# A layer kernel on one core: feed-forward weight steps to and fro, factors through the step, early first units of the next phases

## The chip, the cores and the metric

The kernel runs on one core of a Trainium2 chip. A core has TensorE (PE, matrix products; PEld is its loading of weights), VectorE (DVE), ScalarE (ACT), GpSimd (POOL) and SyncE (SP), which in this kernel issues nearly all transfers. Engines run their own instructions in order and wait for each other by semaphores; an engine's transfers go out in the order in which it issues them. The metric is the device time of one launch in microseconds (us), lower is better.

## The reference

One inference step of a layer: 2048 new tokens behind 16 meta tokens, and 8 running sequences of 4 tokens. Two branches (a state space layer, a gated delta rule) are merged and projected, and a dense gated channel mixer follows. The change concerns the merge's end and what comes after it, in float32:

```
mix = (sigmoid(ga) * br_a + sigmoid(gb) * br_b) @ w_out
x = x + rms_norm(mix, norm_mix_post)
f = rms_norm(x, norm_ffn_pre)                      # 2080 tokens x 1024
f = (silu(f @ w_ffn_gate) * (f @ w_ffn_up)) @ w_ffn_down     # 1024 -> 2816 -> 1024
x = x + rms_norm(f, norm_ffn_post)
```

## The kernel before, in words

Every product of two float32 matrices is made as three products: each operand is split in a rounded part (`xh`, `ah`, `wh`, `hh`, by an ACT copy) and a rest (`xl`, `al`, `wl`, `hl`, by a DVE or POOL subtraction), and hi by hi, lo by hi and hi by lo are summed in PSUM (`mm3`, lines 157 to 159).

The stages, in time: the input projection and the two branches; the merge (`p2_products`), which writes `mg_d` in memory; the way out (`way_out`: `way_rows` multiplies with `w_out`, `way_tail` normalises, adds, normalises again, writes `y_prompt` and has `to_dram` transpose the rows, `pst`, and write them to `f_d` in column form, `fo`); gate and up (`gate_up`), which reads `f_d` as `fr` and writes the gated product to `h_d`; and down, which reads `h_d` as `hr` and `w_ffn_down` as `wr` (`wload`), and sums in `psr`. In the way out, a group is two row tiles of 128 tokens.

Gate and up takes the tokens in three pairs of column blocks (348, 348 and 344 wide, `PAIRS`) and, for each, the weights in 11 steps of 256 columns. A step makes two 2 by 2 block products (gate, i = 0, and up, i = 1) with seven block products each instead of eight, from sums and differences of blocks, in the order a11, a12, s2, s1, s3, a22, s4. A block product is 4 times three matmuls, so a step is 2 x 7 x 12 = 168 matmuls on tiles `psf`.

- `b_parts` loads the four blocks of a token pair (`fr`), forms t1 to t4 on DVE and splits seven operands: eleven DVE operations on 128x1392. For the next pair it is a generator that the last step of a pair advances at its `more()` calls. Its results have one buffer each.
- `a_parts` loads two weight blocks of 1 MB for a step (`araw`, two buffers), forms s1 to s4 on DVE (`S`) and splits: of each matrix a11/a12 and s2/s1 on DVE, s3/s4 and a22 on POOL. It is called for the next step before a step's own code; the split factors lie in a ring of 50 KB a partition (`ar`).
- `gate_up_step`: `sn` is an ACT copy of a product that is needed later, `su` a DVE sum, `th` the tanh gate (ACT, then DVE), `hm` the gated product (mostly POOL), stored by SP.

A scheduler places the instructions, by the order in which the code emits them and by its own estimates; the order on an engine is therefore not that of the text. Pools with `reuse_waits="tile"` may lie over memory of an earlier stage: a tile waits for what lay there.

Down has, for each half of the tokens, four groups of 6, 6, 5 and 5 row blocks of `w_ffn_down`; a block is loaded into one of two `wr` buffers, its rounded half made by ACT, the two halves of the rest by POOL and DVE (lines 142, 144, 145).

The pools around the change, before:

```
                self.tm = self.pool("tm2", 3, ph, **kw)
...
            self.ar = ar.ring(50 * 1024, name="ar")
            self.ar.tile([P, 3072], F32, name="pad")
...
            self.wr = self.pool("wr3", 2, ph, **kw)
            self.wp.add(self.pool("wp3", 12, ph, **kw), 12)
```

Of the kernel before, what the change touches and what calls it, by code (L numbers as in the profile page):

```python
# [7 lines left out]
F32 = mybir.dt.float32  # L8
# [7 lines left out]
P = 128  # L16
# [54 lines left out]
class Trunk:  # L71
# [57 lines left out]
    def wload(self, parts, eng=0):  # L129

        nc = self.nc
        hi = self.wp.tile([P, 1024], F32R, tag="wh", name="wh")
        lo = self.wp.tile([P, 1024], F32R, tag="wl", name="wl")
# [135 lines left out]
    def to_dram(self, ys, gain):  # L269
# [4 lines left out]
        for k0 in range(0, 8, 2):  # L274
# [8 lines left out]
            nc.sync.dma_start(ap_of(self.f_d, k0 * P * XW + c0, [[XW, P], [P * XW, 2], [1, w]]), ft[:, :, :w])  # L283
# [988 lines left out]
    def p2_products(self, b, prep, part, ws):  # L1272
# [4 lines left out]
        for q in range(2):  # L1277
# [27 lines left out]
            nc.sync.dma_start(ap_of(self.mg_d, r0 + b * BLK, [[XW, P], [1, BLK]]), tb[:, 0:BLK])  # L1305
            if b == 0:
                nc.sync.dma_start(ap_of(self.mg_d, r0 + SEQ, [[XW, P], [1, SMP]]), tb[:, BLK:BLK + SMP])
# [116 lines left out]
    def b_parts(self, c0, w):  # L1424
# [7 lines left out]
        def parts(nm, t):  # L1432
            pool = self.xp if nm in ("b11", "b21") else self.xq
# [29 lines left out]
    def a_parts(self, s):  # L1463

        nc, v, gp = self.nc, self.nc.vector, self.nc.gpsimd
        out = [{}, {}]
        def parts(i, names, x, eng):
# [3 lines left out]
            hf, lf = [t.rearrange("p a k m -> p (a k) m") for t in (hi, lo)]  # L1471
            nc.scalar.activation(hf, x, AF.Copy)  # L1472
            eng.tensor_sub(lf, x, hf.bitcast(F32))  # L1473
            for j, nm in enumerate(names):
                out[i][nm] = hi[:, j], lo[:, j]
        raws = []
        for i, w in enumerate((self.w_fg, self.w_fu)):
            raw = self.gr.tile([P, 8, 256], F32, tag="raw", name="araw")
            nc.sync.dma_start(raw, ap_of(w, 256 * s, [[FF, P], [P * FF, 8], [1, 256]]))
            parts(i, ("a11", "a12"), raw[:, :, 0:P], v)  # L1480
            raws.append(raw)
        sums = []
        for i, raw in enumerate(raws):
            a, c = raw[:, :, 0:P], raw[:, :, P:256]
            S = self.gs.tile([P, 4, 4, P], F32, tag="S", name="S")
            v.tensor_add(S[:, 1], c[:, 0:4], c[:, 4:8])  # L1486
            v.tensor_sub(S[:, 2], a[:, 0:4], c[:, 0:4])
            v.tensor_sub(S[:, 0], S[:, 1], a[:, 0:4])  # L1488
            v.tensor_sub(S[:, 3], a[:, 4:8], S[:, 0])
            sums.append(S.rearrange("p a k m -> p (a k) m"))  # L1490
            parts(i, ("s2", "s1"), sums[i][:, 0:8], v)
        for i, raw in enumerate(raws):
            parts(i, ("s3", "s4"), sums[i][:, 8:16], gp)
            parts(i, ("a22",), raw[:, 4:8, P:256], gp)
        return out

    def gate_up(self):
        nc, v = self.nc, self.nc.vector
        xs = self.b_parts(*PAIRS[0])
        B = None  # L1500
        for B in xs:
            pass
        A = self.a_parts(0)
        last = FF // 256 - 1
        for pi, (c0, w) in enumerate(PAIRS):
# [424 lines left out]
```

## Time and profile before

| | |
|---|---|
| median of 3 runs | 3311.0 us (3310.6 to 3314.44) |
| profiled execution | 3310.43 us, span 3308.7 us |
| mean clock of PE | 0.975 |
| PE busy | 3112.5 us (94%) |
| last matmul of the way out's products | starts at 1802 us |
| gate and up, first to last matmul | 1822.7 to 2777.0 us |
| down, first matmul | 2787.1 us |

Times are counted from the span's start. A row in time has its start, its length, the engine, the line, the operation, the tiles (out<-in) and, in brackets, how long the engine had been idle before it and what released it. A row of a group has the number of instructions after x, their summed time, the mean of one in ns, and the idle time before them. `SPq` and `POOLq` are issues of transfers by these engines.

### The profile page before, as it was taken

How to read it: one execution, taken by the hardware profiler on the slowest of the kernel's cores; microseconds unless marked ns; L12 is line 12 of the kernel's file. 1: busy time of each engine (PE TensorE's matmuls, PEld its weight loads, DVE VectorE, ACT ScalarE, POOL GpSimd, SP SyncE). 2: the span in 40 equal slices, each digit the busy share in tenths (PEclk: the TensorE clock that was granted, in tenths of full speed). 3: DMA queues.
4: the chain of work that ended last, by engine and by line, in shares of the span. 5: the costliest groups of instructions: out<-in, count | busy, mean ns of one | idle time of the engine just before them, and what ended most of it. 6: DMA issues, size and time to landing. Idle time of an engine off the chain costs nothing. (4 is left out here: it accounts for less than half of the span.)

```text
span 3308.7 us, 47381 instructions
## 1 busy us (share of the span) xinstructions
PE 3112.5 (94%) x17461; PEld 2721.0 (82%) x17461; DVE 2078.1 (63%) x4672; ACT 1125.2 (34%) x1960; POOL 888.5 (27%) x835
## 2 busy tenths in 40 slices
PE   6998999999999998999998799999999998999998
PEld 5887878877777777988776799999989997888886
DVE  6888854657887546553454767777776774236235
ACT  4633222433332224221243434434443443313211
POOL 1123431123232212101000344444453443212110
PEclk9999999999999999999999899999999999999999
DMA  5336465545465435653553423343332334326223
GB/s 117 122 100 183 118 171 163 123 119 148 143 193 161 125 111 162 194 153 125 160 186 139 141 95 104 107 136 103 103 100 85 107 110 131 123 86 163 78 64 69
DMA packets 483224, 423.48 MB, mean 128 GB/s; under 512 B 122906, under 2 KB 407642, under 8 KB 482992
## 3 DMA queue, kind: packets, MB, share of 16 engines
q1 hardware_dynamic: 478288, 403.42, 41.3%
q0 software_dynamic: 4704, 17.04, 2.3%
q8 instruction: 137, 2.24, 0.3%
q14 instruction: 95, 0.78, 0.1%
HBM read 292.46 MB, written 127.65 MB: 127 GB/s over the span
## 5 line engine op out<-in xcount | busy, mean ns | idle before, releaser
L157 PE MATMUL psf<-xh,ah 128*128 128x348 f32 (+1 forms) x1848 | 603.6, 327 | 35.4 <-ACT sn L1525 30.8
L159 PE MATMUL psf<-xh,al 128*128 128x348 f32 (+1 forms) x1848 | 597.6, 324 | 17.0 <-DVE al L1473 17.0
L158 PE MATMUL psf<-xl,ah 128*128 128x348 f32 (+1 forms) x1848 | 595.7, 322 | 0.0
L144 POOL TENSOR_TENSOR wl<-wr,wh 128x512 fp32r<-128x512 f32 x136 | 221.8, 1634 | 892.0 <-ACT wh L142 811.0
L157 PEld LDWEIGHTS psf<-xh,ah 128*128 128x128 f32 x1848 | 350.7, 190 | 49.5 <-ACT sn L1525 44.3
L159 PEld LDWEIGHTS psf<-xh,al 128*128 128x128 f32 x1848 | 350.6, 190 | 18.5 <-DVE al L1473 18.5
L158 PEld LDWEIGHTS psf<-xl,ah 128*128 128x128 f32 x1848 | 350.7, 190 | 0.0
L157 PE MATMUL psg<-pgh,wh 128*128 128x512 f32 (+1 forms) x800 | 301.0, 376 | 1.3 <-ACT wh L142 1.3
L1621 PE MATMUL psr<-wh,hh 128*128 128x512 f32 (+2 forms) x748 | 291.2, 391 | 9.8 <-ACT wh L142 9.8
L159 PE MATMUL psg<-pgh,wl 128*128 128x512 f32 (+1 forms) x800 | 291.6, 365 | 4.9 <-DVE wl L145 4.1
L1622 PE MATMUL psr<-wl,hh 128*128 128x512 f32 (+2 forms) x748 | 292.3, 391 | 3.0 <-POOL wl L144 3.0
L158 PE MATMUL psg<-pgl,wh 128*128 128x512 f32 (+1 forms) x800 | 292.1, 365 | 0.0
L1624 PE MATMUL psr<-wh,hl 128*128 128x512 f32 x704 | 274.3, 390 | 0.0
L142 ACT ACTIVATE wh<-wr 128x1024 fp32r<-128x1024 f32 x136 | 143.1, 1056 | 256.8 <-PE psg L158 58.9
L1473 POOL TENSOR_TENSOR al<-S,ah 128x1024 fp32r<-128x1024 f32 x66 | 162.8, 2467 | 228.4 <-ACT ah L1472 130.8
L145 DVE TENSOR_TENSOR wl<-wr,wh 128x512 fp32r<-128x512 f32 x136 | 114.8, 845 | 147.3 <-ACT wh L142 146.5
L1472 ACT ACTIVATE ah<-araw 128x1024 fp32r<-128x1024 f32 (+1 forms) x132 | 110.7, 840 | 224.6 <-DMA araw<-w_ffn_up 106.2
L1472 ACT ACTIVATE ah<-S 128x1024 fp32r<-128x1024 f32 x132 | 135.8, 1051 | 142.2 <-DVE S L1488 124.3
L157 PE MATMUL psq<-pgh,wh 128*128 128x512 f32 (+1 forms) x480 | 181.9, 379 | 0.4 <-ACT pgh L264 0.3
L159 PEld LDWEIGHTS psg<-pgh,wl 128*128 128x128 f32 x800 | 156.1, 195 | 31.1 <-issue 4.6
L157 PEld LDWEIGHTS psg<-pgh,wh 128*128 128x128 f32 x800 | 156.4, 196 | 24.7 <-issue 3.6
L158 PEld LDWEIGHTS psg<-pgl,wh 128*128 128x128 f32 x800 | 156.5, 196 | 22.0 <-issue 2.6
(490 smaller groups left out, 6826.6 us busy)
## 6 DMA issues: line engine op xcount, KB each, us to landing
wr<-w_in SPq DMA_DIRECT2D x72, 512.0 KB
araw<-w_ffn_gate SPq DMA_DIRECT2D x33, 1024.0 KB
araw<-w_ffn_up SPq DMA_DIRECT2D x33, 1024.0 KB
wr<-w_ffn_down SPq DMA_DIRECT2D x44, 512.0 KB
zg_d<-gt SPq DMA_DIRECT2D x80, 256.0 KB
h_d<-hm SPq DMA_DIRECT2D x44, 348.0 KB
qkv_d<-cy SPq DMA_DIRECT2D x48, 256.0 KB
hr<-h_d SPq DMA_DIRECT2D x16, 768.0 KB
```

What stands on the lines that cost most here:

```text
L142: nc.scalar.activation(hi[:, :n], raw[:, :n], AF.Copy)
L144: nc.gpsimd.tensor_sub(lo[:, :c], raw[:, :c], hi[:, :c].bitcast(F32))
L145: nc.vector.tensor_sub(lo[:, c:n], raw[:, c:n], hi[:, c:n].bitcast(F32))
L157: t.matmul(ps, wh, xh, start=first, stop=False, **kw)
L158: t.matmul(ps, wh, xl, start=False, stop=False, **kw)
L159: t.matmul(ps, wl, xh, start=False, stop=last, **kw)
L1472: nc.scalar.activation(hf, x, AF.Copy)
L1473: eng.tensor_sub(lf, x, hf.bitcast(F32))
L1621: nc.tensor.matmul(ps, hi[:, k, cl], wh[:, cs], start=k == 0, stop=False)
L1622: nc.tensor.matmul(ps, hi[:, k, cl], wl[:, cs], start=False, stop=both and k == n - 1)
L1624: nc.tensor.matmul(ps, lo[:, k, c - c0:c - c0 + r], wh[:, cs], start=False, stop=k == n - 1)
```

## The change

- The stores of the way out to `f_d` and of the merge to `mg_d` are issued by GpSimd instead of SP.
- The pairs pass over the weight steps to and fro: 0 to 10, 10 to 0, 0 to 10. At a change of pair the step is the same, and its factors are kept: `a_parts` runs 31 times instead of 33.
- `a_parts` is a generator that the step advances by `fac()` at six places, with what is left at the step's end. `S` of four blocks becomes `S` (s2, s1) and `R` (s3, s4).
- Pools: `su` has 3 buffers instead of 4, `th` 2 instead of 3, the ring `ar` 56 KB instead of 50 with 24 KB of padding instead of 12, `tm2` 4 buffers instead of 3; t1 and t2 have a pool of their own (`xr`).
- Down's pools lie otherwise: `wr` and ten of the `wh` and `wl` pairs (now one tile, `wu`) on the right side, over memory of `ar`, `araw` and others; two pairs, `hh` and `hr` on the left.

How the order moves, at three places. New lines carry numbers 3 to 16 higher for the same code. On DVE, from the last rows of the way out (`wa`) into the first step: the splits of the first token pair (`xl`, with `fr` and `t` for the sums) and of the first two factors (`al<-araw` of gate and up). Before:

```order
L1407 TENSOR_SCALAR wa<-xr,wrs 128x1024 x2
L1486 TENSOR_TENSOR S<-araw 128x512
L1487 TENSOR_TENSOR S<-araw 128x512
L1488 TENSOR_TENSOR S<-S,araw 128x512
L1489 TENSOR_TENSOR S<-araw,S 128x512
L1446 TENSOR_TENSOR fr<-fr 128x1392
L1473 TENSOR_TENSOR al<-araw,ah 128x1024
L1449 TENSOR_TENSOR t_17730<-fr 128x1392
L1437 TENSOR_TENSOR xl<-fr,xh 128x1392
```

And the rows that follow it, up to the second `al`:

```order
L1454 TENSOR_TENSOR fr<-fr 128x1392
L1437 TENSOR_TENSOR xl<-t_17730,xh 128x1392
L1437 TENSOR_TENSOR xl<-fr,xh 128x1392 x2
L1458 TENSOR_TENSOR t_17730<-fr,t_17730 128x1392
L1473 TENSOR_TENSOR al<-araw,ah 128x1024
```

After:

```order
L1411 TENSOR_SCALAR wa<-xr,wrs 128x1024 x2
L1450 TENSOR_TENSOR fr<-fr 128x1392
L1453 TENSOR_TENSOR t_17733<-fr 128x1392
L1441 TENSOR_TENSOR xl<-fr,xh 128x1392
L1458 TENSOR_TENSOR fr<-fr 128x1392
L1441 TENSOR_TENSOR xl<-t_17733,xh 128x1392
L1441 TENSOR_TENSOR xl<-fr,xh 128x1392 x2
L1462 TENSOR_TENSOR t_17733<-fr,t_17733 128x1392
L1476 TENSOR_TENSOR al<-araw,ah 128x1024 x2
```

The first `al` stood between the token operations and stands behind them now; four operations on `S` and `R` have moved ahead, in among the roots of the last rows.

On POOL, one plain step of the first pair, from the `hm` that ends the step before. Before:

```order
L1576 TENSOR_TENSOR hm<-th,su 128x348
L1473 TENSOR_TENSOR al<-S,ah 128x1024
L1473 TENSOR_TENSOR al<-araw,ah 128x512
L1551 TENSOR_TENSOR hm<-th,su 128x348
L1564 TENSOR_TENSOR hm<-th,su 128x348
L1473 TENSOR_TENSOR al<-S,ah 128x1024
L1473 TENSOR_TENSOR al<-araw,ah 128x512
```

After:

```order
L1589 TENSOR_TENSOR hm<-th,su 128x348
L1476 TENSOR_TENSOR al<-R,ah 128x1024
L1562 TENSOR_TENSOR hm<-th,su 128x348
L1576 TENSOR_TENSOR hm<-th,su 128x348
L1476 TENSOR_TENSOR al<-araw,ah 128x512
L1476 TENSOR_TENSOR al<-R,ah 128x1024
L1476 TENSOR_TENSOR al<-araw,ah 128x512
```

Three of the four splits now stand behind the step's own `hm` and one ahead of them. A weight buffer is free after its `al<-araw`, so the loads' issues move to the end of a step.

On SP, the end of gate and up and the first loads of down. Before:

```order
L1479 DMA araw<-w_ffn_up 128x8x256
L1538 DMA h_d<-hm 128x688 x2
L1732 DMA row<-norm_ffn_post 128x1024
L1538 DMA h_d<-hm 128x688
L1605 DMA hr<-h_d 128x6x256
L1538 DMA h_d<-hm 128x688
L1605 DMA hr<-h_d 128x6x256
L140 DMA wr<-w_ffn_down 128x1024 x2
L1605 DMA hr<-h_d 128x6x256 x2
L140 DMA wr<-w_ffn_down 128x1024 x8
```

After:

```order
L1482 DMA araw<-w_ffn_up 128x8x256
L1547 DMA h_d<-hm 128x688 x2
L144 DMA wr<-w_ffn_down 128x1024
L1547 DMA h_d<-hm 128x688 x2
L144 DMA wr<-w_ffn_down 128x1024
L1621 DMA hr<-h_d 128x6x256 x2
L1547 DMA h_d<-hm 128x688
L1750 DMA row<-norm_ffn_post 128x1024
L1547 DMA h_d<-hm 128x688
L144 DMA wr<-w_ffn_down 128x1024 x8
```

Two loads of weights and two of `hr` have moved ahead of the last two stores of `h_d`; the other weights stay behind them.

The diff, cut:

```diff
...
-    def wload(self, parts, eng=0):
+    def wload(self, parts, one=False):
         nc = self.nc
-        hi = self.wp.tile([P, 1024], F32R, tag="wh", name="wh")
-        lo = self.wp.tile([P, 1024], F32R, tag="wl", name="wl")
+        if one:
+            both = self.wp.tile([P, 2, 1024], F32R, tag="wu", name="wu")
+            hi, lo = both[:, 0], both[:, 1]
+        else:
+            hi = self.wp.tile([P, 1024], F32R, tag="wh", name="wh")
+            lo = self.wp.tile([P, 1024], F32R, tag="wl", name="wl")
         raw = self.wr.tile([P, 1024], F32, tag="wr", name="wr")
...
                 nc.scalar.activation(ft[:, kt - k0, :w], ps[:, kt - k0, :w], AF.Copy, scale=gain[:, kt:kt + 1])
-            nc.sync.dma_start(ap_of(self.f_d, k0 * P * XW + c0, [[XW, P], [P * XW, 2], [1, w]]), ft[:, :, :w])
+            nc.gpsimd.dma_start(ap_of(self.f_d, k0 * P * XW + c0, [[XW, P], [P * XW, 2], [1, w]]), ft[:, :, :w])
             yield
...
             r0 = m * P * XW
-            nc.sync.dma_start(ap_of(self.mg_d, r0 + b * BLK, [[XW, P], [1, BLK]]), tb[:, 0:BLK])
+            nc.gpsimd.dma_start(ap_of(self.mg_d, r0 + b * BLK, [[XW, P], [1, BLK]]), tb[:, 0:BLK])
             if b == 0:
-                nc.sync.dma_start(ap_of(self.mg_d, r0 + SEQ, [[XW, P], [1, SMP]]), tb[:, BLK:BLK + SMP])
+                nc.gpsimd.dma_start(ap_of(self.mg_d, r0 + SEQ, [[XW, P], [1, SMP]]), tb[:, BLK:BLK + SMP])
             yield
...
         def parts(nm, t):
-            pool = self.xp if nm in ("b11", "b21") else self.xq
+            pool = self.xp if nm in ("b11", "b21") else self.xr if nm in ("t1", "t2") else self.xq
             hi = pool.tile([P, 4, GW], F32R, tag=nm + "h", bufs=1, name="xh")[:, :, :w]
...
-    def a_parts(self, s):
+    def a_parts(self, s, out):
         nc, v, gp = self.nc, self.nc.vector, self.nc.gpsimd
-        out = [{}, {}]
+        flat = lambda t: t.rearrange("p a k m -> p (a k) m")
         def parts(i, names, x, eng):
...
             lo = self.ar.tile([P, n, 4, P], F32R, name="al")
-            hf, lf = [t.rearrange("p a k m -> p (a k) m") for t in (hi, lo)]
-            nc.scalar.activation(hf, x, AF.Copy)
-            eng.tensor_sub(lf, x, hf.bitcast(F32))
+            nc.scalar.activation(flat(hi), x, AF.Copy)
+            eng.tensor_sub(flat(lo), x, flat(hi).bitcast(F32))
             for j, nm in enumerate(names):
                 out[i][nm] = hi[:, j], lo[:, j]
-        raws = []
+        raws, sums = [], [None] * 2
         for i, w in enumerate((self.w_fg, self.w_fu)):
...
             nc.sync.dma_start(raw, ap_of(w, 256 * s, [[FF, P], [P * FF, 8], [1, 256]]))
-            parts(i, ("a11", "a12"), raw[:, :, 0:P], v)
             raws.append(raw)
-        sums = []
-        for i, raw in enumerate(raws):
-            a, c = raw[:, :, 0:P], raw[:, :, P:256]
-            S = self.gs.tile([P, 4, 4, P], F32, tag="S", name="S")
+        def early(i):
+            a, c = raws[i][:, :, 0:P], raws[i][:, :, P:256]
+            S = self.gs.tile([P, 2, 4, P], F32, tag="S", name="S")
+            R = self.gs.tile([P, 2, 4, P], F32, tag="R", name="R")
             v.tensor_add(S[:, 1], c[:, 0:4], c[:, 4:8])
-            v.tensor_sub(S[:, 2], a[:, 0:4], c[:, 0:4])
             v.tensor_sub(S[:, 0], S[:, 1], a[:, 0:4])
-            v.tensor_sub(S[:, 3], a[:, 4:8], S[:, 0])
-            sums.append(S.rearrange("p a k m -> p (a k) m"))
-            parts(i, ("s2", "s1"), sums[i][:, 0:8], v)
-        for i, raw in enumerate(raws):
-            parts(i, ("s3", "s4"), sums[i][:, 8:16], gp)
-            parts(i, ("a22",), raw[:, 4:8, P:256], gp)
-        return out
+            v.tensor_sub(R[:, 0], a[:, 0:4], c[:, 0:4])
+            v.tensor_sub(R[:, 1], a[:, 4:8], S[:, 0])
+            parts(i, ("s2", "s1"), flat(S), v)
+            sums[i] = flat(R)
+        def late(i):
+            parts(i, ("s3", "s4"), sums[i], gp)
+            parts(i, ("a22",), raws[i][:, 4:8, P:256], gp)
+        for i in range(2):
+            parts(i, ("a11", "a12"), raws[i][:, :, 0:P], v)
+            yield
+        for f in (early, late):
+            for i in range(2):
+                f(i)
+                yield
     def gate_up(self):
-        nc, v = self.nc, self.nc.vector
-        xs = self.b_parts(*PAIRS[0])
+
+        n = FF // 256
         B = None
-        for B in xs:
+        for B in self.b_parts(*PAIRS[0]):
             pass
-        A = self.a_parts(0)
-        last = FF // 256 - 1
-        for pi, (c0, w) in enumerate(PAIRS):
-            nxt = None
-            for s in range(last + 1):
-                An = self.a_parts((s + 1) % (last + 1)) if s < last or pi < 2 else None
-                if s == last and pi < 2:
-                    nxt = self.b_parts(*PAIRS[pi + 1])
-                Bn = self.gate_up_step(s, c0, w, A, B, nxt)
-                A = An
-            B = Bn
-
-    def gate_up_step(self, s, c0, w, A, B, nxt):
+        A = [{}, {}]
+        for _ in self.a_parts(0, A):
+            pass
+        order = [(pi, s) for pi in range(3) for s in (range(n) if pi != 1 else range(n - 1, -1, -1))]
+        for (pi, s), (pj, sn) in zip(order, order[1:] + [(3, -1)]):
+            An, ga = A, None
+            if pj < 3 and sn != s:
+                An = [{}, {}]
+                ga = self.a_parts(sn, An)
+            nxt = self.b_parts(*PAIRS[pj]) if pi < pj < 3 else None
+            Bn = self.gate_up_step(s, *PAIRS[pi], A, B, nxt, ga)
+            A, B = An, Bn or B
+
+    def gate_up_step(self, s, c0, w, A, B, nxt, ga):
         nc, v, gp = self.nc, self.nc.vector, self.nc.gpsimd
...
         def plus(ps, t):
-            o = self.gt.tile([P, GW], F32, tag="su", bufs=4, name="su")[:, :w]
+            o = self.gt.tile([P, GW], F32, tag="su", bufs=3, name="su")[:, :w]
             v.tensor_add(o, ps, t)
...
         def gated(g):
-            t = self.gt.tile([P, GW], F32, tag="th", bufs=3, name="th")[:, :w]
+            t = self.gt.tile([P, GW], F32, tag="th", bufs=2, name="th")[:, :w]
             nc.scalar.activation(t, g, AF.Tanh, scale=0.5)
...
         more = lambda: next(nxt) if nxt else None
+        fac = lambda: next(ga, None) if ga else None
         s1, s2, s3 = [None] * 2, [None] * 2, [None] * 2
...
             prod(X[i], i, "a12", "b21", True)
+            fac()
         Bn = more()
...
             s3[i] = snap(Y[i])
+            fac()
         more()
...
             prod(Z[i], i, "s4", "b22")
+            fac()
             if i == 0:
...
         out(0)
+        if ga:
+            for _ in ga:
+                pass
         return Bn
...
             for gi, (k0, n) in enumerate(KGROUPS):
-                wd = [self.wload([(ap_of(self.w_fd, (k0 + k) * P * D, [[D, P], [1, D]]), 0, D, 0)])
+                wd = [self.wload([(ap_of(self.w_fd, (k0 + k) * P * D, [[D, P], [1, D]]), 0, D, 0)], True)
                       for k in range(n)]
...
                 self.ac = self.pool("ac", 2, ph, **kw)
-                self.tm = self.pool("tm2", 3, ph, **kw)
+                self.tm = self.pool("tm2", 4, ph, **kw)
                 self.sq = self.pool("sq", 1, ph, **kw)
...
             ar = self.pool("ar", 1, ph, side="right", **kw)
-            self.ar = ar.ring(50 * 1024, name="ar")
-            self.ar.tile([P, 3072], F32, name="pad")
+            self.ar = ar.ring(56 * 1024, name="ar")
+            self.ar.tile([P, 6144], F32, name="pad")
             self.gt = self.pool("gt", 1, ph, **kw)
             self.xq = self.pool("xq", 1, ph, **kw)
+            self.xr = self.pool("xr", 1, ph, **kw)
             self.gs = self.pool("gs", 1, ph, **kw)
...
             self.wp = Ring()
-            self.wr = self.pool("wr3", 2, ph, **kw)
-            self.wp.add(self.pool("wp3", 12, ph, **kw), 12)
-            self.hr = self.pool("hr", 2, ph, **kw)
-            self.hh = self.pool("hh", 2, ph, **kw)
             self.ac = self.pool("ac3", 9, ph, **kw)
...
             self.small = self.pool("small3", 2, ph, **kw)
+            self.wr = self.pool("wr3", 2, ph, side="right", **kw)
+            self.wp.add(self.pool("wp3", 10, ph, side="right", **kw), 10)
+            self.wp.add(self.pool("wp5", 2, ph, **kw), 2)
+            self.hh = self.pool("hh", 2, ph, **kw)
+            self.hr = self.pool("hr", 2, ph, **kw)
             self.down()
...
```

## The prediction

> **What bounds the kernel now.** I read the page's head first, then a table of the gate and up stage by stretches, then, at each place where TensorE (PE) falls behind, its groups, waits and rows in time. PE is busy for 94% of the span and nothing else comes near it:
>
> ```profile
> span 3308.7 us, 47381 instructions
> PE 3112.5 (94%) x17461; PEld 2721.0 (82%) x17461; DVE 2078.1 (63%) x4672; ACT 1125.2 (34%) x1960; POOL 888.5 (27%) x835
> ```
>
> So only the places where PE waits are to be had. The stage has 33 steps (3 token pairs by 11 weight steps) of 168 matmuls. The stretches below are step 0; steps 1 to 9; 10 and 11 (a pair change); 12 to 20; 21 and 22 (the other change); 23 to 32; and two plain steps alone, 13 and 30. The columns are length, then busy time of PE, PEld, DVE, ACT, POOL, then clock, DMA share and GB/s.
>
> ```profile
> 1822.70:1867.50 44.80, 31.29 (x168) 30.04 (x169) 35.83 (x34) 20.77 (x26) 12.67 (x6) 0.80 0.50 163
> 1867.50:2117.15 249.65, 244.05 (x1514) 241.15 (x1513) 177.12 (x207) 101.34 (x162) 106.34 (x63) 1.00 0.32 102
> 2117.15:2185.40 68.25, 58.21 (x338) 56.32 (x337) 55.23 (x57) 31.55 (x43) 33.84 (x14) 0.92 0.43 137
> 2185.40:2435.05 249.65, 244.27 (x1514) 241.07 (x1513) 177.16 (x207) 101.55 (x162) 106.24 (x63) 1.00 0.32 102
> 2435.05:2502.99 67.94, 58.28 (x338) 57.14 (x337) 55.06 (x57) 31.20 (x43) 33.68 (x14) 0.92 0.30 94
> 2502.99:2777.20 274.21, 269.25 (x1682) 264.30 (x1680) 195.18 (x223) 107.64 (x176) 117.16 (x70) 1.00 0.30 97
> 2212.88:2240.32 27.44, 27.09 (x169) 26.80 (x169) 19.62 (x23) 11.22 (x18) 11.75 (x7) 1.00 0.33 103
> 2694.50:2721.37 26.87, 26.84 (x169) 26.42 (x169) 20.04 (x23) 11.10 (x18) 11.77 (x7) 1.00 0.32 106
> ```
>
> Nine steps take 249.65 us, 27.74 each. Each pair change costs two steps 68.25 and 67.94 instead of 55.5: 12.8 and 12.4 too much, or 13.4 and 13.1 against steps like 13 and 30, which have no late load. The first step costs 17.4 too much against step 13.
>
> In a plain step PE stops once. Rows in time of PE, ACT, DVE, POOL and SP of step 13, which starts at 2212.9:
>
> ```profile
> 2222.30 0.32 PE L159 MATMUL psf<-xh,al 128*128 128x348 f32 x1
> 2222.97 0.43 PE L157 MATMUL psf<-xh,ah 128*128 128x348 f32 x1 [0.35 <-ACT sn L1525]
> 2222.47 0.44 ACT L1525 ACTIVATE sn<-psf 128x348 f32<-128x348 f32 x1
> 2215.49 1.76 DVE L1486 TENSOR_TENSOR S<-araw 128x512 f32<-128x512 f32 x1 [1.90 <-POOL al L1473]
> 2221.47 0.51 DVE L1529 TENSOR_TENSOR su<-psf,sn 128x348 f32<-128x348 f32 x1
> 2216.67 1.38 POOL L1576 TENSOR_TENSOR hm<-th,su 128x348 f32<-128x348 f32 x1
> 2221.38 2.43 POOL L1473 TENSOR_TENSOR al<-S,ah 128x1024 fp32r<-128x1024 f32 x1 [3.33 <-ACT ah L1472]
> ```
>
> Matmuls follow each other at 0.16 us, here at 0.67: the copy `sn` (for a buffer of products) came late, behind a `th` that waited for `su`, which stood on DVE behind the whole split of a weight factor. That is 0.5, and the matmul itself, 0.43 for 0.32, is 0.1 longer: the step loses 0.6 us. In some steps a load makes it worse. Step 17 starts at 2323.2; SP, ACT and PE there:
>
> ```profile
> 2335.70 0.37 SPq L1479 DMA_DIRECT2D araw<-w_ffn_up  x1
> 2340.96 0.63 ACT L1472 ACTIVATE ah<-araw 128x512 fp32r<-128x512 f32 x1 [6.40 <-DMA araw<-w_ffn_up]
> 2341.99 0.43 PE L157 MATMUL psf<-xh,ah 128*128 128x348 f32 x1 [0.76 <-ACT sn L1525]
> ```
>
> The second weight load is issued 12.5 us into the step, once POOL has freed its buffer; ACT, which could have gone on 6.4 us before, waits till it has landed after 5.26 us, and the next `sn` behind it is late for PE.
>
> **The change, part by part.** The sum is made against the profiled execution, 3310.4 us (its span of 3308.7 and 1.7 around it), 0.6 below the median of 3311.0.
>
> *To and fro.* At the two pair changes the weight factors of the last step are kept. Two of 33 `a_parts` go: four loads of 1 MB, and at each change on DVE four `al` and eight `S`. DVE's group of token work in steps 10 and 11, and its groups of factor work in the nine plain steps from 12 on:
>
> ```profile
> L1437 DVE TENSOR_TENSOR xl<-fr,xh 128x1392 fp32r<-128x1392 f32 x5 | 7.9, 1595 | 0.0
> L1473 DVE TENSOR_TENSOR al<-S,ah 128x1024 fp32r<-128x1024 f32 x18 | 22.1, 1226 | 7.5 <-ACT ah L1472 7.0 <-PE psf L159 0.4
> L1488 DVE TENSOR_TENSOR S<-S,araw 128x512 f32<-128x512 f32 x18 | 13.3, 739 | 0.0
> ```
>
> The 55.23 us of DVE hold 11 operations on 128x1392 at about 1.6 (17.6) and two sets of factors. A set is 4 `al` at 1.23 and 8 `S` at 0.74, or some at 1.76 (row at 2215.49): 10.8 to 15 us. Without one set 40 to 44 us stand against 54.9 of PE, and step 10 has its 17.6 and the `su` and `th` alone. In the new order each new token part comes ahead of its first product, so the two steps should run at the plain pace: -26 for both. The ends: -27 and, if the token parts alone hold PE up, half, -13.
>
> *Factors ordered through the step.* POOL is now given `hm`, then the `al<-R` of the second matrix, and only at the step's end the other three. From the step's start su 0.51, hm 1.38 (up to 1.85), al 2.43, two `R` at 0.74 (the price of `S`, the row before), su 0.51, th and sn 0.44, and some 0.1 at each change of engine: 7.8 us, where PE needs `sn` at 9.5 (2222.4 less 2212.9). If both `R` took the 1.76 of `S` beside POOL it would be 9.8. So the 0.6 should mostly go: 18 plain steps of pairs 1 and 2 by 0.6, ten of pair 3, estimated at two thirds of that, make 14.8. I take -10, between 0 and -15, nearer to the uncontended rows since POOL has nothing to do beside these `R`.
>
> *Earlier weight loads.* Step 13, without a late load, takes 27.44. Nine such would take 247.0, so each row of 249.65 holds 2.7 us of late loads; ten like step 30, of 26.87, make 268.7, so the row of 274.21 holds 5.5. Together 10.9. The loads are now issued some 23 and 28 us into a step of 27.4, and used 3.6 and 7.3 us into the next. At 5.26 us for a landing they come some 3 and 1 us early, where the second came late, and PE feels a late one only through the copies behind it. I take -9.5, between -5 and -11.
>
> *From the way out to the first step.* PE, SP and DVE in time, before:
>
> ```profile
> 1822.70:1844.30 21.60, 8.12 (x32) 6.90 (x32) 0.00 (x0) 0.44 (x1) 0.66 0.56 178
> 1819.53 0.36 SPq L1430 DMA_DIRECT2D fr<-f_d  x1
> 1824.42 1.61 DVE L1446 TENSOR_TENSOR fr<-fr 128x1392 f32<-128x1392 f32 x1 [2.52 <-DMA fr<-f_d]
> 1834.21 6.34 DVE L1437 TENSOR_TENSOR xl<-fr,xh 128x1392 fp32r<-128x1392 f32 x2
> 1840.48 2.66 DVE L1458 TENSOR_TENSOR t<-fr,t 128x1392 f32<-128x1392 f32 x1
> 1843.07 1.21 DVE L1473 TENSOR_TENSOR al<-araw,ah 128x1024 fp32r<-128x1024 f32 x1
> 1836.47 5.21 POOL L1473 TENSOR_TENSOR al<-araw,ah 128x512 fp32r<-128x512 f32 x2
> ```
>
> PE has done 32 matmuls when the second `al` ends at 1844.3. Now both first `al` come after the last `t`: PE cannot have done its first 24, which costs 24 by 0.16 = 3.8. Two `S` and `R` that now stand ahead of the last rows' root on DVE add 2 by 0.74 = 1.5, since the load of the last tokens still waits for the last transposes. Against this, POOL has no `al` yet to run beside the two `xl` and `t`, which took 9.0 where three alone take 4.8: up to -4.2. Ends +1 and +5, with a load landing late +8 and with less work ahead of it -1; I take +3.
>
> *The way down.* PE after the last product tile, with SP and POOL in time:
>
> ```profile
> 2777.20:2797.20 20.00, 9.19 (x30) 0.66 0.88 292
> 2797.20:2817.20 20.00, 18.05 (x79) 1.00 0.52 161
> 2817.20:2837.20 20.00, 20.00 (x90) 1.00 0.57 182
> 2782.34 0.81 SPq L140 DMA_DIRECT2D wr<-w_ffn_down  x2
> 2787.14 3.42 POOL L144 TENSOR_TENSOR wl<-wr,wh 128x512 fp32r<-128x512 f32 x2 [8.24 <-ACT wh L142]
> 2795.57 3.51 POOL L144 TENSOR_TENSOR wl<-wr,wh 128x512 fp32r<-128x512 f32 x2 [5.01 <-ACT wh L142]
> ```
>
> At 90 matmuls in 20 us, 60 and 11 are missing: 71 by 0.222 = 15.8 us lost. Weights come two at a time (two buffers), a round taking 2795.57 - 2787.14 = 8.4. The first two are now loaded in the stage's last two steps, and their halves made by its end, so one round of three goes; the next round still starts when the last `h_d` is issued. Hence -8.4 at most. If PE's clock stays low for the six matmuls of each unit that come one by one, it is half of that; I take -7.5, ends -4 and -8.5.
>
> *Stores on GpSimd.* A store to `f_d` issued by SP lets ACT go on 2.7 us after its issue (1817.45 to 1820.16, two rows); GpSimd's own stores take 3.1, and ACT has 3.52 us over in a group of two row tiles:
>
> ```profile
> 1817.45 1.39 SPq L283 DMA_DIRECT2D f_d<-fo  x2
> 1820.16 1.57 ACT L282 ACTIVATE fo<-pst,c_norm_ffn_pre 128x256 f32<-128x256 f32 x4 [2.00 <-DMA f_d<-fo]
> y_prompt<-xr POOLq DMA_DIRECT2D x14, 512.0 KB, 3.1
> 1761.41 1.06 ACT L1390 ACTIVATE sq<-xr 128x1024 bf16<-128x1024 f32 x1 [3.52 <-DVE xr L1400]
> ```
>
> Two waits of 0.4 more fit into 3.5: nothing. With all of it on the path it would be 0.8 for the last group; ends 0 and +3. On SP nothing that PE waits for stood behind these stores but the two token loads just told. The same holds for the stores to `mg_d`, under a PE that is full.
>
> The Trainium skill speaks against this part. "SBUF — State Buffer" ("SBUF: two separate sides") has GpSimd unable to write the descriptors of its stores while VectorE runs in a two-port mode, and gives a store 3.1 us where it takes 0.62 alone. The row of 3.1 for `y_prompt` may hold such a wait already or not; its 14 stores do not tell. By the skill, an estimate: each store 2.5 us later, which by the working of rival C makes 3261 + 18 + 6 = 3285; by the rows nothing is lost.
>
> Sum: -26 - 10 - 9.5 + 3 - 7.5 + 0 = -50, so 3260.4, and 3261 on the median's footing.
>
> **The rivals.** Most of the gain should come true in the likeliest case: 3246 to 3275.
>
> A. *A new wait in every step* (slower than before). `su` of the first product now stands on DVE behind two `R` that wait for POOL, and those behind `hm` and `al`. POOL's pair of 128x512 took 5.21 instead of 2.6 beside DVE's large operations (row at 1836.47), so a POOL that takes twice its 3.8 us would make `sn` come at 11.6 instead of 7.8. Each us past 9.5 then costs 31 us over the steps; the other terms (-40) and the 15 of the present gaps are used up at 55 / 31 = 1.8 us a step. At 2.1 us the gaps cost 65 against 15 now, and the time is 3311 + 50 - 40 = 3321. Against it: `hm` and `al` at 1.38 and 2.43 ran beside such `S` in step 13.
>
> B. *The token parts alone hold PE up* at the pair changes: 13 less gained, 3274. For it: 11 operations on DVE and ACT in one step; against it, DVE has 10 us over.
>
> C. *The stores hold up the way out.* ACT waits twice in a group for a store to free its buffer. If a store by GpSimd took twice the 3.1 us of `y_prompt`, it would be 3.5 later than one by SP; two make 7.0, less the 3.5 over 3.5 in each of 8 groups, and 7.0 before the load of the last tokens: 3261 + 28 + 7 = 3296. Below 1.7 us later each it costs only the last group. For it: f_d has four stores in a row where `y_prompt` has two; against it, the 3.1 was measured beside the same DVE work. The rule that would do it is the one of the Trainium skill's "SBUF — State Buffer" told above.
>
> D. *The way down gains nothing*: should the first two weights not have landed, their place on SP being behind waiting stores, the round stays: 3269. Its order, two stores of an earlier step between loads, speaks against it.
>
> E. *The first step is worse by another 10*, because ACT now has the first factors behind the token parts: 3271.
>
> **How the numbers follow.** The likeliest case 0.55, A 0.08, B 0.12, C 0.08, D 0.06, E 0.08, and 0.03 for two of them together, about 3290. The terms' ends added up give 3248 and 3299, but they would not all fall alike. A range of 3246 to 3290 holds most of the likeliest case and of B, D and E, and the milder half of C; it leaves out A, the pairs and the rest of C. What this kernel's measurement can tell from no change is 0.2%, 6.6 us. Slower by more is A, 0.08; within it lies a milder A or several rivals together, 0.05; faster has the rest, 0.87.
>
> **What would show it.** Steps 10, 11, 21 and 22 at 27 to 28 us each. In plain steps no wait of PE for `sn`, and 26.8 us. ACT waiting no more for `araw`. The first step ending some 3 us later after the last row tile. Between 2777 and 2817 of the old time, some 34 matmuls more. The forecast is wrong if PE shows a new wait in most steps, for `sn` or for `al`, or if the way out takes more than 24.6 us for two row tiles.

## The result, and the profile after

The changed kernel takes 3290.48 us in the median of 4 runs (3283.95 to 3293.09), the kernel before 3310.8 us beside it: a ratio of 0.9936, with a 95% interval of 0.9917 to 0.9955. It is faster by about 20 us. The forecast was 3261, 50 us less, with a range that ended at 3290. So the direction was right, the size was not, and 30 us of the expected gain were missing. Two of the executions counted below took nearly twice the usual time (6530 us, the kernel before; 5904 us, the last experiment): the ratios leave them out, the medians do not.

The head of the page after, to be read against the one before:

```profile
span 3287.0 us, 47621 instructions
PE 3105.4 (94%) x17461; PEld 2709.1 (82%) x17461; DVE 2015.5 (61%) x4648; ACT 1120.6 (34%) x1944; POOL 910.1 (28%) x903
```

The same 17461 matmuls in 21.7 us less, and PE still at 94%. The stretches show where. They are cut as before: step 0; steps 1 to 9; 10 and 11; 12 to 20; 21 and 22; 23 to 32; and the plain steps 13 and 30 alone. Columns: length, busy time of PE, PEld, DVE, ACT and POOL, clock, DMA share, GB/s.

```profile
1833.40:1870.85 37.45, 30.14 (x168) 29.40 (x169) 34.56 (x33) 19.32 (x27) 15.03 (x8) 0.86 0.48 151
1870.85:2120.85 250.00, 243.52 (x1514) 240.98 (x1513) 167.05 (x207) 104.05 (x162) 110.53 (x65) 1.00 0.33 105
2120.85:2176.20 55.35, 54.12 (x338) 53.55 (x337) 41.91 (x46) 24.61 (x35) 17.57 (x11) 1.00 0.41 128
2176.20:2424.80 248.60, 243.53 (x1514) 240.98 (x1513) 167.18 (x208) 104.15 (x162) 109.07 (x64) 1.00 0.33 103
2424.80:2479.70 54.90, 53.75 (x338) 53.17 (x337) 41.63 (x46) 24.49 (x35) 17.42 (x11) 1.00 0.34 106
2479.70:2753.00 273.30, 267.05 (x1682) 264.48 (x1681) 179.91 (x224) 113.99 (x177) 115.51 (x68) 1.00 0.32 102
2203.74:2231.37 27.63, 27.05 (x170) 26.77 (x169) 18.59 (x24) 11.55 (x18) 12.14 (x8) 1.00 0.33 103
2671.67:2699.10 27.43, 26.72 (x170) 26.44 (x169) 18.53 (x24) 11.52 (x18) 12.12 (x8) 1.00 0.33 103
```

The pair changes are done with: 55.35 and 54.90 where 68.25 and 67.94 stood, 25.9 us. But the three long stretches of plain steps have kept their length: 250.00, 248.60 and 273.30 against 249.65, 249.65 and 274.21, 1.6 us where 19.5 had been expected. Step 13 takes 27.63 instead of 27.44, step 30 27.43 instead of 26.87. What was lost now and then to a late load is lost in every step, as PE's waits for the copy `sn` say (in us, times, the longest). Before, in steps 12 to 20:

```profile
PE psf L157 <- ACT sn L1525: 5.4, 11, 1.5
```

After, in steps 13 to 20, one in each:

```profile
PE psf L161 <- ACT sn L1534: 4.6, 8, 0.6
```

Down, from the last product tile of gate and up to the end, and 200 us in its middle, for the tiles `psr` alone (their columns: PE, PEld, DVE, ACT). Before:

```profile
2777.20:3308.70 531.50, 504.92 (x2210) 409.70 (x2210) 69.82 (x102) 19.84 (x34) 0.98 0.39 106
2900.00:3100.00 200.00, 200.00 (x883) 164.25 (x883) 26.45 (x39) 9.55 (x17) 1.00 0.41 108
```

After:

```profile
2753.00:3287.00 534.00, 516.56 (x2210) 407.79 (x2210) 69.86 (x102) 19.84 (x34) 0.99 0.37 99
2753.00:2773.00 20.00, 15.79 (x62) 11.07 (x63) 0.00 (x0) 0.00 (x0) 1.00 0.59 203
2900.00:3100.00 200.00, 200.00 (x860) 158.38 (x859) 24.59 (x36) 10.52 (x18) 1.00 0.45 120
```

The start is as good as hoped, and better: 62 matmuls in the first 20 us instead of 30. Yet down is 2.5 us longer as a whole. In its middle, where PE waits for nothing and the clock is whole, it does 860 matmuls in 200 us and not 883: 0.2326 us each instead of 0.2265. Over 2210 matmuls that is 13 us, and it is PE at work, so that no view of waits shows it. Nothing in the forecast had a term for it.

In the way out, PE's and ACT's waits, from its first to its last product. Before:

```profile
PE pst L278 <- DVE wa L1407: 5.2, 7, 1.1
ACT fo L282 <- DMA f_d<-fo: 5.4, 7, 1.8
```

After, with one row of ACT in time and the store's time from issue to landing:

```profile
PE pst L282 <- DVE wa L1411: 10.6, 7, 5.7
ACT fo L286 <- DMA f_d<-fo: 17.0, 7, 2.8
1692.21 1.36 ACT L1440 ACTIVATE xh<-fr 128x1392 fp32r<-128x1392 f32 x1 [4.37 <-DMA fr<-f_d]
f_d<-fo POOLq DMA_DIRECT2D x25, 256.0 KB, 4.0
```

A store by GpSimd takes 4.0 us to land. ACT waits three times as long for the buffers, which stays nearly hidden (PE's other six waits are 4.9 us together, 4.1 before); but the first tokens' load, which waits for these stores, is late, ACT stands 4.37 us at the copy that needs it, and one of the seven waits of PE in the way out grows from 1.1 to 5.7 us.

Taken together, by the starts of matmuls in the two traces: projection and branches -5.7 and merge +0.8 (code that did not change; over the seven profiles with the old alignment the first of these stages took 1287.7 to 1302.3 us), way out +6.6, from its last product to the second step +1.7, pair changes -25.9, plain steps -1.6, down +2.5: -21.6.

### The profile page after: what moved, and what is told of

It is laid out like the page before. It is cut to its first block, busy times and chain, and to the rows that moved or that the text cites. A ratio compares the mean times of both kernels' runs of the same rounds, so it can differ in the third digit from the quotient of the medians.

```text
span 3287.0 us, 47621 instructions
## 1 busy us (share of the span) xinstructions
PE 3105.4 (94%) x17461; PEld 2709.1 (82%) x17461; DVE 2015.5 (61%) x4648; ACT 1120.6 (34%) x1944; POOL 910.1 (28%) x903
## 5 line engine op out<-in xcount | busy, mean ns | idle before, releaser
L1638 PE MATMUL psr<-wu,hh 128*128 128x512 f32 (+2 forms) x748 | 295.4, 395 | 4.2 <-POOL wu L148 4.2
L1637 PE MATMUL psr<-wu,hh 128*128 128x512 f32 (+2 forms) x748 | 294.3, 395 | 0.0
L1640 PE MATMUL psr<-wu,hl 128*128 128x512 f32 x704 | 277.6, 395 | 0.0
L148 POOL TENSOR_TENSOR wl<-wr,wh 128x512 fp32r<-128x512 f32 x92 | 143.8, 1563 | 389.5 <-ACT wh L146 318.9
L1476 POOL TENSOR_TENSOR al<-R,ah 128x1024 fp32r<-128x1024 f32 x62 | 162.8, 2626 | 50.4 <-ACT ah L1475 50.4
L1638 PEld LDWEIGHTS psr<-wu,hh 128*128 128x128 f32 (+2 forms) x748 | 137.7, 184 | 42.9 <-POOL wu L148 6.7
L163 PE MATMUL psq<-pgh,wl 128*128 128x512 f32 (+1 forms) x480 | 172.9, 360 | 0.0
L162 PE MATMUL psq<-pgl,wh 128*128 128x512 f32 (+1 forms) x480 | 172.6, 360 | 0.0
L1637 PEld LDWEIGHTS psr<-wu,hh 128*128 128x128 f32 (+2 forms) x748 | 137.6, 184 | 35.9
```

The costliest lines, as they stand in the source:

```text
L148: nc.gpsimd.tensor_sub(lo[:, :c], raw[:, :c], hi[:, :c].bitcast(F32))
L162: t.matmul(ps, wh, xl, start=False, stop=False, **kw)
L163: t.matmul(ps, wl, xh, start=False, stop=last, **kw)
L1476: eng.tensor_sub(flat(lo), x, flat(hi).bitcast(F32))
L1637: nc.tensor.matmul(ps, hi[:, k, cl], wh[:, cs], start=k == 0, stop=False)
L1638: nc.tensor.matmul(ps, hi[:, k, cl], wl[:, cs], start=False, stop=both and k == n - 1)
```

## The experiments

The numbers after a stage's name come from the matmuls' starts in each run's trace; the totals are medians beside runs of the kernel before on the same chip.

**Alignment of down's weights.** By the addresses that the built program gives, ten of the twelve weight tiles now start 32 bytes off a multiple of 64 in their partition (the first at 139232, 2175 times 64 and 32); all of the old ones started at a multiple (the first at 25280). Two kernels turn that round. In the changed kernel:

```diff
         self.const = self.pool("const", 1)
+        self.pool("edge", 1, side="right").tile([P, 8], F32, name="edge")
```

> The changed kernel with 32 bytes taken at the right end of the on-chip memory, so that every tile on the right side starts 32 bytes lower and at a multiple of 64. Theory M (a moving operand that starts 32 bytes off a multiple of 64 makes a matmul of 512 columns slower, 0.2333 instead of 0.2268 us from start to start): down falls from 534 to about 521 us, and the input projection and the merge, whose moving operands stood 32 off in both kernels, gain up to 3456 matmuls by 0.006 = 21 us; in all 25 to 40 us less than the changed kernel, about 3255. Rival T (the rounded half and the rest now lie in one tile, or the weights in the upper part of the memory): nothing changes, 3290.

And in the kernel before:

```diff
+            self.pool("shift", 1, ph, **kw).tile([P, 8], F32, name="shift")
             self.wp.add(self.pool("wp3", 12, ph, **kw), 12)
+            self.pool("back", 1, ph, **kw).tile([P, 8], F32, name="back")
```

> The kernel before with down's weight tiles moved by 32 bytes and nothing else. Theory M: each matmul of down goes from 0.227 to 0.233 us, 2210 of them, so 13 us more: 3324. Rival T: the two halves are in tiles of their own and low in the memory as before, so no change: 3311.

The first took 3279.86 us, ratio to the kernel before 0.9904 (0.9888 to 0.9921), whose interval overlaps that of the changed kernel, so that the stage decides; the second 3320.54, 1.0042 (1.0025 to 1.0058). The same 200 us of down, of the changed kernel aligned:

```profile
2900.00:3100.00 200.00, 200.00 (x884) 162.93 (x883) 25.63 (x38) 10.52 (x18) 1.00 0.45 122
```

and of the kernel before, shifted:

```profile
2900.00:3100.00 200.00, 200.00 (x859) 159.89 (x858) 25.98 (x38) 8.87 (x16) 1.00 0.41 108
```

884 and 859, where 860 and 883 stood: the rate goes with the 32 bytes both ways, and not with the tile or the side. Down takes 521.7 instead of 534.2 us in the one, 546.0 instead of 531.6 in the other. Theory M holds for down as a whole stage, and T falls. Whether it is the start of what PE reads or of what ACT, DVE and POOL write into the same tiles, the two kernels do not separate. The theory's second half, 21 us in the projection and the merge, did not come: there the mean interval fell from 0.233 to 0.231 only, the merge took 299.0 instead of 301.4 us, and what the projection gained, if anything, is below its own scatter of 15 us. Why these matmuls still take 0.231 was not tried.

**Who issues the stores.** The changed kernel with both stores back on SP:

```diff
-            nc.gpsimd.dma_start(ap_of(self.f_d, ...
+            nc.sync.dma_start(ap_of(self.f_d, ...
-            nc.gpsimd.dma_start(ap_of(self.mg_d, ...
+            nc.sync.dma_start(ap_of(self.mg_d, ...
```

> The changed kernel with the stores to f_d and mg_d issued by SP again. Theory Q (stores by GpSimd take 4.0 us to land instead of some 2.5, which makes the first two token loads late, and ACT and DVE wait for these in the middle of the way out): the one gap of 6.1 us in the way out falls to 1.1, and the first step starts 1 to 2 us earlier: 5 to 7 us less than the changed kernel, 3284. Rival: the late token loads come from the order of the transfers, not from who issues the stores: no change.

Median 3281.49, ratio 0.9916 (0.9896 to 0.9936). The total alone does not tell it from the changed kernel, since the intervals overlap; the stage does. The way out takes 201.9 us instead of 208.2, from its last product to the second step 65.85 instead of 67.34, and the two waits are back where they were:

```profile
PE pst L282 <- DVE wa L1411: 5.5, 7, 1.0
ACT fo L286 <- DMA f_d<-fo: 5.8, 7, 2.3
```

So it matters who issues the stores, as theory Q has it, and this part of the change costs 7.7 us. That SP's stores land in some 2.5 us stays an estimate: the trace has no landings for them. The two stores were turned back together; the merge, which holds those to `mg_d`, took 300.9 instead of 301.4 us.

**The one buffer of R.** What PE waits for in each plain step is still `sn`, later than before. PE, DVE and POOL around the start of step 13 of the changed kernel, 2203.74:

```profile
2214.04 0.42 PE L161 MATMUL psf<-xh,ah 128*128 128x348 f32 x1 [0.58 <-ACT sn L1534]
2201.21 2.40 POOL L1476 TENSOR_TENSOR al<-R,ah 128x1024 fp32r<-128x1024 f32 x1 [1.06 <-ACT ah L1475]
2201.49 2.50 DVE L1544 SCALAR_TENSOR_TENSOR th<-th,su 128x348 f32<-128x348 f32 x1 [0.86 <-ACT th L1543]
2203.91 1.78 DVE L1490 TENSOR_TENSOR R<-araw 128x512 f32<-128x512 f32 x1
2206.64 0.51 DVE L1538 TENSOR_TENSOR su<-psf,sn 128x348 f32<-128x348 f32 x1
2207.23 1.32 POOL L1589 TENSOR_TENSOR hm<-th,su 128x348 f32<-128x348 f32 x1 [2.09 <-DVE su L1538]
2208.51 2.85 POOL L1476 TENSOR_TENSOR al<-R,ah 128x1024 fp32r<-128x1024 f32 x1
2211.39 0.69 DVE L1490 TENSOR_TENSOR R<-araw 128x512 f32<-128x512 f32 x1 [2.29 <-POOL al L1476]
```

The `su` that feeds `hm` could run at the step's start, 2203.74. It runs 2.9 us later, because the second matrix's `R` stands ahead of it on DVE and can only be written once POOL has read the first one out of the single buffer (2201.21 to 2203.6). DVE does not stand idle for it: a `th` beside that read takes 2.5 us, to 2204.0, and the `R` follows at once. What the single buffer sets is the `R`'s place, ahead of `su`. From there the chain is the forecast's: `hm`, `al`, again `R` behind `al`, then su, th, sn. One more buffer:

```diff
-            R = self.gs.tile([P, 2, 4, P], F32, tag="R", name="R")
+            R = self.gs.tile([P, 2, 4, P], F32, tag="R", bufs=2, name="R")
```

> The changed kernel with two buffers for R. Theory R (each step's wait of PE at its 60th matmul comes from the second R standing on DVE ahead of su, waiting for POOL to free the one R buffer): the wait of 0.89 us goes, plain steps take 26.8 us instead of 27.63 (26.5 instead of 27.4 in the third pair), about 31 by 0.8 = 25 us less: 3266. Rival W (POOL itself is late: hm and al<-R keep sn late whatever the buffers): the steps stay at 27.6, no change; or another wait of the same size takes its place.

Median 3260.91, ratio 0.9852 (0.9837 to 0.9866). Steps 12 to 20 with two buffers:

```profile
2160.35:2401.50 241.15, 241.15 (x1514) 241.15 (x1513) 173.79 (x208) 107.12 (x162) 104.91 (x64) 1.00 0.34 106
```

PE's waits for `sn` in all steps after the first, of the changed kernel and, from 1870 us on, with two buffers:

```profile
PE psf L161 <- ACT sn L1534: 20.2, 31, 1.9
PE psf L161 <- ACT sn L1534: 0.2, 1, 0.2
```

And DVE in step 13 with two buffers, which starts at 2187.16:

```profile
2187.75 0.51 DVE L1538 TENSOR_TENSOR su<-psf,sn 128x348 f32<-128x348 f32 x1
2189.92 2.89 DVE L1490 TENSOR_TENSOR R<-araw 128x512 f32<-128x512 f32 x1
2194.06 0.52 DVE L1538 TENSOR_TENSOR su<-psf,sn 128x348 f32<-128x348 f32 x1
```

The first `su` now runs 0.6 us into the step, ahead of every `R`, and the `sn` at the chain's end starts 7.9 us into it, near the forecast's 7.8. 241.15 instead of 248.60, and PE busy throughout; 26.79 us a plain step, 26.47 in the third pair; all steps after the first 27.9 us shorter. Theory R is shown, as far as the one buffer goes: with a second one the scheduler also orders DVE's work otherwise, and what the wait and what the place of `R` are worth was not told apart. Rival W falls: POOL does the same work in the same order.

**To and fro alone**, in the kernel before:

```diff
-            for s in range(last + 1):
-                An = self.a_parts((s + 1) % (last + 1)) if s < last or pi < 2 else None
+        order = [(pi, s) for pi in range(3) for s in (range(n) if pi != 1 else range(n - 1, -1, -1))]
+        for (pi, s), (pj, sn) in zip(order, order[1:] + [(3, -1)]):
+            An = A
+            if pj < 3 and sn != s:
+                An = self.a_parts(sn)
...
```

> The kernel before with the to and fro order and the kept factors, and nothing else of the change. Theory P (at a pair change the DVE could not make a set of factors and the token parts in one step): steps 10 and 11, and 21 and 22, fall from 68 to 55 us each pair, 26 us in all, 3283; the late weight loads and the 0.67 us waits stay. Rival B of the prediction (the token parts alone hold PE up): 13 us less, 3296.

Median 3296.23, ratio 0.9971 (0.9961 to 0.9982). Steps 10 and 11:

```profile
2120.00:2153.05 33.05, 29.14 (x170) 28.27 (x169) 22.68 (x21) 11.71 (x16) 10.36 (x6) 0.95 0.30 92
2153.05:2180.05 27.00, 27.00 (x170) 26.79 (x169) 19.53 (x25) 13.76 (x20) 5.55 (x5) 1.00 0.46 150
```

The second step of the change is free, the first still takes 33 us; the two changes together give 16.5 us in this profile, not 26 and not 13. The total gives 9.6 us by the ratio (6 to 13). Theory P's 26 is out by both; rival B's 13 lies between them, and why the total gives less than the stage is open. PE's waits in step 10, and ACT and PE at the longest of them:

```profile
PE psf L157 <- ACT sn L1524: 2.5, 2, 2.1
PE psf L159 <- POOL al L1473: 1.4, 1, 1.4
2138.71 1.36 ACT L1436 ACTIVATE xh<-t 128x1392 fp32r<-128x1392 f32 x1 [5.44 <-DVE t L1449]
2139.98 0.44 ACT L1524 ACTIVATE sn<-psf 128x348 f32<-128x348 f32 x1
2140.47 0.42 PE L157 MATMUL psf<-xh,ah 128*128 128x348 f32 x1 [2.11 <-ACT sn L1524]
```

The copy `sn` stands on ACT behind the rounded half of a token part, `t`: rival B's mechanism, though smaller than priced. The mean clock is 0.95 in this step and 1.00 in the changed kernel's, and near the end an `al` of POOL comes late. In the changed kernel's step 10 PE waits twice for `sn`, 0.6 and 0.7 us. The token parts themselves stand no earlier there: this `t` ends 18.7 us into the step here and 19.0 there. So the other 9.5 us of the pair changes came with the rest of the change, its orders, buffers and pools; which of them it was not tried.

**Does the generator order the factors?** The changed kernel with all of `a_parts` emitted before the step's code:

```diff
-                ga = self.a_parts(sn, An)
+                for _ in self.a_parts(sn, An):
+                    pass
```

> The changed kernel with all of a_parts emitted at the start of the step, as before the change, and everything else of the change kept. Theory N (the order through the step comes from the buffers and the scheduler, not from the places where the generator is advanced): plain steps 27.6 and 27.4 us, no late weight load, as in the changed kernel. Rival: without the generator the steps go back to 27.44 with late loads in a third of them.

One run, 3292.27 us. Plain steps take 27.63 and 27.43, the steps after the first 881.3 us in all (882.0 in the changed kernel). The order of instructions is that of the changed kernel on PE, ACT, POOL and SP, and on DVE one `su` stands three rows later. The generator does nothing here; the scheduler, given `S` and `R` in tiles of their own, the longer ring and the new pools, puts the factors where they are. Which of these does it was not tried.

**The corrections together.** The edge tile, two buffers for R and the stores on SP:

> The changed kernel with three corrections together: 32 bytes at the right end (weights at a multiple of 64), two buffers for R, the stores on SP again. If the three causes are separate, their gains add: down -12.5, plain steps -28, way out and first step -8, so 48 us less than the changed kernel, 3241. Rival: they share slack (a DVE that is earlier meets a DMA that is later), 3250 to 3260.

Median 3235.57, ratio 0.9797 (0.9779 to 0.9816). Down 522.2, steps 854.1, way out 201.6, then 65.0 to the second step: the three gains add up. By the ratios it is 0.0139 of 3309, 46 us, less than the changed kernel, against a sum of 48.

Then the first weight step's factors ahead of the first token parts in `gate_up`:

```diff
+        A = [{}, {}]
+        for _ in self.a_parts(0, A):
+            pass
         B = None
         for B in self.b_parts(*PAIRS[0]):
             pass
-        A = [{}, {}]
-        for _ in self.a_parts(0, A):
-            pass
```

> As e7_three, and the code emits the first weight step's factors ahead of the first token parts, which puts the first two al on DVE ahead of the second sum of the tokens. Theory F (PE could not do its first 24 matmuls because both first al came behind all token work): first step and boundary 3 to 5 us shorter than in e7_three, 3237. Rival G (the late load of the last tokens bounds the first step, whatever the order of al): no change.

Median 3236.03, ratio 0.9795 (0.9779 to 0.9812). The stage says yes, 60.9 us from the last product of the way out to the second step instead of 65.0; the total does not show these 4 us. What held PE in the changed kernel, DVE and PE in time:

```profile
1835.15 3.12 DVE L1441 TENSOR_TENSOR xl<-fr,xh 128x1392 fp32r<-128x1392 f32 x2
1838.18 3.75 DVE L1462 TENSOR_TENSOR t<-fr,t 128x1392 f32<-128x1392 f32 x1
1841.86 4.50 DVE L1476 TENSOR_TENSOR al<-araw,ah 128x1024 fp32r<-128x1024 f32 x2
1844.19 0.66 PE L163 MATMUL psf<-xh,al 128*128 128x348 f32 x1 [6.79 <-DVE al L1476]
```

And token tiles 352 wide:

```diff
-GW = 348
+GW = 352
```

> As e7_three, with the token tiles 352 wide instead of 348 (the work stays 348), so that in gate and up every moving operand starts at a multiple of 64 bytes instead of at 0, 16, 32 and 48 in turn. Theory M, if it holds for any start off 64: 5544 matmuls by some 0.001 us less, 6 us, 3235. Rival: only operands whose length is a multiple of 64 bytes pay for a start off it; gate and up's steps stay at 26.8 and 26.5 us.

Median 3237.16, ratio 0.9793 (0.9774 to 0.9813). Plain steps 26.61 and 26.32 instead of 26.77 and 26.41, all steps after the first 849.4 instead of 854.1: 4.7 us of the 6, again below what the total can tell. So the layout of tiles with slices of 1392 bytes costs something too, though less (0.0009 us a matmul on the mean). That each operand pays for its own start is not shown: in the kernel with three corrections, by the program's addresses, slices of 348 columns that started at a multiple of 64 took 0.160 us to the next matmul and the others 0.159.

All five:

> All corrections together: right side at a multiple of 64 bytes, two buffers for R, stores on SP, the first factors ahead of the first token parts, token tiles 352 wide. By the stages of the earlier runs: steps 849.4, down 521.5, first step and boundary 61, way out 201.8; 9 us less than e7_three, 3227, and 75 to 80 less than the kernel before. Rival: the corrections meet in the first step (order and width), and it stays at e7_three's 3236.

Median 3229.45, ratio 0.9756 (0.9734 to 0.9778), 80 us less than the 3308.98 of the kernel before beside it. By stages: way out 201.6, then 61.9, steps 849.7, down 521.9.

## Why the prediction was wrong, point by point

- *To and fro, -26*: measured -25.9. The size was right, in part by luck: the kept factors alone gave 16.5 in the profile, less by the total, and the rest came with the other parts of the change. The working counted all of it to the factors kept and took the new order for granted.
- *Factors ordered through the step, -10, and earlier loads, -9.5*: measured -1.6 for both. This is the step that failed first and most, by 18 of the 33 us that the changed stages fell short of the sum. The loads do come early: ACT waits for none of them in the plain steps. But the chain to `sn`, worked out to 7.8 us, took its start from a `su` that runs at the step's first moment. On DVE that `su` stands behind the second `R`, whose place comes from POOL's reading of the first in the one buffer: 2.9 us. With them `sn` starts at 2213.55, 9.8 us into the step, and is read at 10.3 instead of 9.5. The gap did not go from 0.6 to nothing: against the steps with two buffers it went to 0.84, and to 0.96 in the third pair. It is rival A, a new wait in every step, in a milder form than the one priced: A named the `R` behind `hm` and `al`, not the `R` before them. The second buffer gave 27.9 us, more than the 19.5 once hoped for.
- *From the way out to the first step, +3*: +1.7 from the last product to the second step, and near the forecast by luck: 1.5 of it went when the stores went back to SP. The order of the factors did what was told. PE's first run was held until 1844.2, the end of the first `al`, behind the last `t`, and emitting these factors first gave 4.0, the 3.8 of the working. With the stores on SP only +0.2 was left (65.85 against 65.62), so nearly as much was saved elsewhere. The rows show a part of it: the two `xl` took 3.1 instead of 6.3 us, as the working hoped, but the `t` behind them 3.75 instead of 2.66, with POOL's `al` beside it.
- *The way down, -7.5*: the start gained 10.2 us, by the 60th matmul. What was missing is no wait at all: each of the 2210 matmuls became 0.006 us slower, as ten of the twelve weight tiles moved to 32 bytes off a multiple of 64. The sum had no term for this: it took a move of memory to cost nothing once its waits were priced.
- *Stores on GpSimd, 0*: 7.7 us, rival C in a mild form. The landing was 4.0 us, where the row of `y_prompt` had 3.1. The slack of 3.52 us a group did cover ACT's waits for its buffers, as argued; but the working looked at two loads only, those at the end, and said that nothing else behind the stores mattered. The first two loads of token columns, in the middle of the way out, depend on the stores too, and ACT waits for them in order. The Trainium skill's "SBUF — State Buffer" ("SBUF: two separate sides") gave the right direction. Whether its cause, GpSimd held off by VectorE, is at work no run here shows: only that PE and ACT waited longer with stores by GpSimd than with stores by SP.
- The sum with the measured terms: -25.9 - 1.6 + 1.7 + 6.6 - 10.2 + 12.7 = -16.7, and -4.9 from stages that did not change.

## What to carry to other kernels

Where a tile is given its own buffer, write down who must have read it before it is written again, and where that writer stands in its engine's queue: a single buffer between two engines that take turns can hold both up, and here the order in which the code was written did not change that. When pools move, look at the address modulo 64 of the tiles that the matrix engine streams, and at matmuls per microsecond in a stretch without waits, before and after; a busy engine at 100% hides a loss of 3%. And when a store moves to another queue, follow every load that reads it, not only the last.

## What the runs showed of the hardware that was not expected

- In down, a matmul with a moving operand (the one that is streamed) of 512 float32 columns follows the one before after 0.2265 us if all the weight tiles start at a multiple of 64 bytes, and after 0.2326 us if ten of twelve, or all, start 32 bytes off (883 and 884 against 860 and 859 in 200 us, in two kernels each way). In gate and up, with 348 columns, four starts in turn against a multiple of 64 made 0.0009 us on the mean.
- It is not a price that each matmul pays by its own start alone. Two of the twelve weight buffers of the changed kernel were at a multiple of 64 and still took 0.232 us on the mean, among neighbours that were not; and the matmuls of the merge kept 0.231 when all their moving operands started at a multiple. That stays unexplained.
- A store of 256 KB issued by GpSimd landed 4.0 us after its issue in the median, where one of 512 KB by the same queue took 3.2 in the same stage.
